# Splitting two operand sums before they go through memory, and adding the residual by DMA

## The chip, the cores and the metric

The kernel runs on one core of a Trainium2 chip. The metric is the device time of one execution in microseconds (us). TensorE (PE) multiplies, VectorE (DVE) and ScalarE (ACT) work on tiles, GpSimd (POOL) and SyncE (SP) here mostly issue DMA transfers between the core's memory and the chip's.

## The reference, cut to what matters

The block is a mixer (a state-space branch and a short convolution, merged by gates) with a residual, a norm, and then an MLP with a squared ReLU, a residual and a final norm. The change is in the MLP and its residual.

```
h = h + mixer_block(rmsnorm(h, g1), ...)
xn = rmsnorm(h, g2)                         # 1024 x 1024
f = relu(xn @ w_ff1); f = f * f             # 1024 x 4096
h = h + f @ w_ff2                           # 1024 x 1024
out = rmsnorm(h, g_final)
```

## The kernel before

All tensors are float32. TensorE works on the faster fp32r type, so each operand is cut into a high part (a rounded copy made by ScalarE) and a low part (the operand minus the high part, made by VectorE), and a product is three matmuls: high by high, high by low, low by high.

The MLP's two products are computed in **groups** by a scheme of the Strassen kind: a group multiplies a 2x2 block of weights by a 2x2 block of the operand with seven block products P1 to P7 instead of eight. One block product is a **chain** of 12 matmuls of 128x512 (4 blocks of the inner dimension, three matmuls each). Groups 0 to 13 belong to the first product, groups 14 to 25 to the second, and one slab of the inner dimension is multiplied in the plain way, in 16 chains (`pf`) between group 13 and group 14. The last stage (`pl`) adds another plain slab, the residual, and the final norm.

`seven(g, after)` issues one group in the order P1, P4 of the group before, P5, P2, P6, P3, P7. P1 is copied by ScalarE into the bank `seed` with its sign turned, and P6, P7 and P4 add to it there. Results leave the banks as quadrants in `done`: c11 after P2, c12 after P3, c22 after P7, c21 after P4. P4 writes into the bank that c22 is read from, so it waits for VectorE's c22. Behind each chain `after(i)` is called (i from 0 to 6), which issues the cutting and loading that other groups need. Each engine runs its own instructions in the order in which the program issues them; nothing else sets the order.

The weights of a group come as two raw tiles (`group_load`, SP). `w_parts` forms two sums of them (steps s1, s2), their high parts (h0 to h3) and low parts (l0 to l3); the tables `FIRST` and `SECOND` say behind which chain of the group before (first list) and of the group itself (second list) each step is issued. In the first product, sum 1 serves P5 and P6, sum 2 serves P3 and P7, part 0 serves P1 and P2, part 3 serves P4. In the second product part 0 serves P2 and P4.

The squared quadrants of the first product are the operands of the second: B11, B12, B21, B22 and the sums t1, n2, t3, t4 formed from them in `done`. POOL stores each to memory (`out_of`, 256 KB each) and SP loads it back per chunk of four groups (`x_load`, two loads of 512 KB each per name); `x_cut` cuts it (two ScalarE copies, two VectorE subtractions of 128x1024). The second product has three chunks; a boundary between chunks lies at groups 17 to 18 and 21 to 22. The residual h lies in memory as `hd`, written long before; eight tiles `ha` are loaded from it ahead of the plain slab, and every quadrant of the second product is added into them by VectorE.

In the rows, gs, gh and gl are a group's sum, high and low part, ha the accumulated output, xl1B and the like low parts of the second product's operands (the digit is the chunk), fh and fl those of a plain slab, hw and lw those of a plain slab's weights, holda, holdb, holdc the tiles for quadrants and sums of the first product.

Of the kernel before, what the change touches and what calls it, by code (L numbers as in the profile page):

```python
# [39 lines left out]


X_OF = {"P1": "B11", "P5": "t1", "P2": "B21", "P6": "n2", "P3": "B22", "P7": "t3", "P4": "t4"}


@with_exitstack
def block_kernel(ctx, tc, x_t, par, ssm, w_u, win, wco, wglu, wo, w1, w2, out):
# [632 lines left out]
    def ssm_z():  # L679
# [31 lines left out]
    hd = [dram.tile([P, S], F32, tag=f"hd{i}", name=f"hd{i}") for i in range(8)]  # L711
    h2d = {i: dram.tile([P, S], F32, tag=f"h2d{i}", name=f"h2d{i}") for i in range(8 * N_CHUNK, DFF // P)}
    xd = {
        (q, nm): dram.tile([P, 4, HALF], F32, tag=f"xd{q}{nm}", name=f"xd{q}{nm}")
        for q in range(N_CHUNK) for nm in X_OF.values()
    }

    def load_x(i):
# [276 lines left out]
    def four(t):  # L995
        return t.rearrange("p (a k m) -> p a k m", a=2, k=4)
# [29 lines left out]
    def w_parts(g):  # L1026

        (r0, r1), w = gw[g]["raw"], gw[g]
        second = g >= N_GROUP
        a11, a22 = r0[:, 0], r1[:, 1]  # L1030
        a12, a21 = (r1[:, 0], r0[:, 1]) if second else (r0[:, 1], r1[:, 0])
        full, single = (r1, a11) if second else (r0, a22)
        src = {"0": full, "3": single}
        of = {"1": ("P5", "P6"), "2": ("P3", "P7"), "0": ("P2", "P4") if second else ("P1", "P2"),
              "3": ("P1",) if second else ("P4",)}
        hi, lo = {}, {}

        def tile_for(kind, nm):
            if nm == "3":
                return half(f"g{kind}3_{g}", F32R).rearrange("p (k m) -> p k m", k=4)  # L1040
            return (u4 if second and nm != "1" else l4)(f"g{kind}{nm}_{g}")

        def sums(nm):
            t = four(unit(f"gs{nm}_{g}")) if g == 0 else wpool.tile(
                [P, 8, P], F32, tag="w", name=f"gs{nm}_{g}").rearrange("p (a k) m -> p a k m", a=2)
            src[nm] = t
            if nm == "1":
                V.tensor_add(t[:, 0], a21, a22)
                V.tensor_add(t[:, 1], t[:, 0], a11)
            else:  # L1050
                V.tensor_add(t[:, 0], src["1"][:, 1], a12)
                V.tensor_add(t[:, 1], a11, a21)  # L1052

        def high(nm):
            hi[nm] = tile_for("h", nm)
            A.activation(hi[nm], src[nm], AF.Copy)  # L1056

        def lower(nm):
            lo[nm] = tile_for("l", nm)
            V.tensor_sub(lo[nm], src[nm], hi[nm].bitcast(F32))  # L1060
            for i, name in enumerate(of[nm]):
# [8 lines left out]
                gw[g]["do"]["shl".index(what[0])](what[1])  # L1070
            yield

    FIRST = ["s1 h0", "s2 h1 l0", "h2 l1", "l2"], ["", "", "h3", "l3"]
    SECOND = ["", "", "", "s1 h3", "h1 l3", "l1"], ["s2 h0", "l0 h2", "l2"]

    def group_steps(g, own):
# [51 lines left out]
        next(rms[1])  # L1128

    def group_first():  # L1130
        next(prep0)
        next(prep0)

    group_load(0)
    prep0 = group_steps(0, 0)
# [39 lines left out]
    xq = {}  # L1175

    def x_load(q, name):
        ts = []
        for u in range(2):
            t = unit(f"xl{q}{name}{u}", F32R)  # L1180
            nc.sync.dma_start(t.bitcast(F32), xd[q, name][:, 2 * u:2 * u + 2, :].rearrange("p k t -> p (k t)"))
            ts.append(t)
        xq[q, name] = ts

    def x_cut(q, name):
        ops = []
        for u, t in enumerate(xq[q, name]):
            hi = unit(f"xh{q}{name}{u}", F32R)
            A.activation(hi, t.bitcast(F32), AF.Copy)
            low.append((t, t.bitcast(F32), hi))  # L1190
            lows(1)
            ops.append((hi, t))
        lows()
        xq[q, name] = ops
# [4 lines left out]
    def seven(g, after):  # L1199

        seed = seeds[g % 2]
        pa, pe = bank(f"pa{g}"), bank(f"pe{g}")
        chain(pa, g, "P1", True)
        A.activation(seed, pa, AF.Copy, scale=-1.0)  # L1204
        after(0)
        if g not in (0, N_GROUP):
            last_product(g - 1)
        after(1)
        chain(pe, g, "P5", True)
        s5, v2 = half(f"s5_{g}"), half(f"v2_{g}")  # L1210
# [12 lines left out]
        done(g, "c22", seed, s5)
        after(6)
# [7 lines left out]
    def done(g, quad, ps, less):  # L1232
# [8 lines left out]
        paired = g >= 2  # L1241
        q, c = divmod(g - 2, 4)

        def out_of(name, t):
            nc.gpsimd.dma_start(xd[q, name][:, c, :], t)

        hold = held.setdefault(g, {})
        if paired and quad == "c11":
# [21 lines left out]
        if quad == "c12":  # L1270
            t1 = hold["b"][:, HS[0]]
            V.tensor_sub(t1, hold["a"][:, HS[0]], t)
            out_of("t1", t1)
        elif quad == "c22":
            t3, n2 = hold["b"][:, HS[1]], hold["c"][:, HS[1]]
            V.tensor_sub(t3, hold["a"][:, HS[1]], t)
            out_of("t3", t3)
            V.tensor_sub(n2, hold["a"][:, HS[0]], t3)
            out_of("n2", n2)
        elif quad == "c21":  # L1280
            t4 = half(f"t4_{g}")
            V.tensor_sub(t4, t, hold["c"][:, HS[1]])
            out_of("t4", t4)

    plain_slab = 2 * N_CHUNK

    for g in range(N_GROUP):
        last_g = g == N_GROUP - 1
        if g == 0:
            for _ in prep0:  # L1290
                pass
        preps = [group_steps(g, 1), group_steps(g + 1, 0) if not last_g else iter(())]

        def after(i):
            for prep in preps:
                next(prep, None)
            if i == 4 and g + 2 < N_GROUP:
                group_load(g + 2)
            if last_g:
                if i == 2:  # L1300
                    slab_load(plain_slab)
                elif 3 <= i:
                    slab_cut(plain_slab, i - 3)
                if i == 4:
                    w2_cut(4 * plain_slab)

        seven(g, after)
    last_product(N_GROUP - 1)


    h = []
    for e in range(8):
        t = late.tile([P, S], F32, tag="l", name=f"ha{e}")
        nc.sync.dma_start(t, hd[e])
        h.append(t)

    names_x = list(X_OF.values())
    g0 = N_GROUP
# [1 line left out]
    for j in range(16):  # L1320
        n, ii, hh = 4 * plain_slab + j // 4, (j // 2) % 2, j % 2
        if j % 4 == 0 and j < 12:
            w2_cut(n + 1)
        if j == 9:
            group_load(g0)
            prep = group_steps(g0, 0)
        e = 2 * (j // 4) + ii
        p = bank(f"pf{n}_{ii}_{hh}")
        products(p, w2p[n], range(4 * ii, 4 * ii + 4), slab[plain_slab], HS[hh])
        V.tensor_add(h[e][:, HS[hh]], p, h[e][:, HS[hh]])  # L1330
        if j % 2 and j < 12:
            x_load(0, names_x[j // 2])
            if j > 1:
                x_cut(0, names_x[j // 2 - 1])
        if j >= 10:
            next(prep, None)
    group_load(g0 + 1)

    for g in range(g0, g0 + 4 * N_CHUNK):
        q, e = divmod(g - g0, 4)  # L1340
# [3 lines left out]
        def after(i):  # L1344
            if e == 0:
                if q == 0:
                    if i == 0:
                        x_cut(0, "t3")
                        x_load(0, "t4")
                    elif i == 2:  # L1350
                        x_cut(0, "t4")
                elif i == 0:
                    x_cut(q, "B22")
                elif i == 1:
                    x_load(q, "t4")
                elif i == 2:
                    x_cut(q, "t3")
                elif i == 4:
                    x_cut(q, "t4")
            if e == 3 and not final:  # L1360
                if i != 1:
                    x_load(q + 1, names_x[max(i - 1, 0)])
                if i >= 3:
                    x_cut(q + 1, names_x[i - 3])
            if final:
                if i == 0:
                    slab_load(n_slab - 1)
                if i in (2, 4):
                    for k in range(3) if i == 2 else (3,):
                        n = 4 * (n_slab - 1) + k  # L1370
                        w2p[n] = raw_load(w2[n], f"w2_{n}")
                if i >= 2:
                    if i < 6:
                        slab_cut(n_slab - 1, i - 2)
                    if i > 2:
                        n = 4 * (n_slab - 1) + i - 3
                        w2p[n] = cut(w2p[n], f"w2_{n}", blocks8)
            for prep in preps:
                next(prep, None)
            if i == 6:  # L1380
# [106 lines left out]
```

## Time and profile before

| what | value |
|---|---|
| median of 3 runs | 1485.74 us (1485.54 to 1486.83) |
| profiled execution | 1487.28 us, of which the span from the first to the last instruction is 1485.5 us |
| busy in the span | PE 1450.2 us (98%), DVE 1008.4 (68%), ACT 545.1 (37%), POOL 131.3 (9%) |
| mean granted TensorE clock | 0.991 |
| traffic | 144.31 MB, mean 97 GB/s |

Busy time is the sum over an engine's instructions. A PE that is busy can still be slow, since the granted clock stretches a matmul; the clock is given as a share of full speed.

### The profile page before, as it was taken

How to read it: one execution, taken by the hardware profiler on the slowest of the kernel's cores; microseconds unless marked ns; L12 is line 12 of the kernel's file. 1: busy time of each engine (PE TensorE's matmuls, PEld its weight loads, DVE VectorE, ACT ScalarE, POOL GpSimd, SP SyncE). 2: the span in 40 equal slices, each digit the busy share in tenths (PEclk: the TensorE clock that was granted, in tenths of full speed). 3: DMA queues.
4: the chain of work that ended last, by engine and by line, in shares of the span. 5: the costliest groups of instructions: out<-in, count | busy, mean ns of one | idle time of the engine just before them, and what ended most of it. 6: DMA issues, size and time to landing. Idle time of an engine off the chain costs nothing.

```text
span 1485.5 us, 16929 instructions
## 1 busy us (share of the span) xinstructions
PE 1450.2 (98%) x6563; PEld 1200.9 (81%) x6563; DVE 1008.4 (68%) x1573; ACT 545.1 (37%) x776; POOL 131.3 (9%) x306
## 2 busy tenths in 40 slices
PE   9989999999999999999999999999999999998997
PEld 7868888888888888888888878888887787887887
DVE  6678487776877776347536866766666657767565
ACT  6541432223232238324213443333324224344354
POOL 5840000000000000000010001222111000000000
PEclk9999999999999999999999999999999999999999
DMA  5111111101111111114312233444458516162302
GB/s 215 29 43 43 43 43 50 48 32 56 43 43 43 43 43 35 65 57 156 135 43 94 78 105 123 153 156 148 151 169 347 169 53 232 57 217 94 114 28 87
DMA packets 44096, 144.31 MB, mean 97 GB/s; under 512 B 5488, under 2 KB 9968, under 8 KB 44016
## 3 DMA queue, kind: packets, MB, share of 16 engines
q1 hardware_dynamic: 34736, 112.82, 22.6%
q0 software_dynamic: 9280, 30.42, 5.3%
q8 instruction: 51, 0.84, 0.2%
q14 instruction: 29, 0.24, 0.1%
HBM read 108.61 MB, written 34.60 MB: 96 GB/s over the span
## 4 chain that ended last, share of the span: by engine, by line
PE 83%; DVE 9%; ACT 4%; DMA 2%; issue 2%; SPq 0%; DVEq 0%; ACTq 0%
PE ps L134 8%; PE ps L136 8%; PE ps L135 8%; PE seed L1088 4%; PE seed L1090 4%; PE seed L1089 4%; PE pa L1090 3%; PE pa L1089 3%; PE pa L1088 3%; PE pe L1090 3%; PE pe L1089 3%; PE pe L1088 3%; PE pc L134 2%; PE pg L136 2%; PE pg L135 2%; PE pc L136 2%
## 5 line engine op out<-in xcount | busy, mean ns | idle before, releaser
L134 PE MATMUL ps<-xh,wh 128*128 128x512 f32 x656 | 259.8, 396 | 1.2 <-ACT wh L94 1.2
L136 PE MATMUL ps<-xh,wl 128*128 128x512 f32 x656 | 256.1, 390 | 2.2 <-DVE wl L95 2.2
L135 PE MATMUL ps<-xl,wh 128*128 128x512 f32 x656 | 255.3, 389 | 0.0
L136 PEld LDWEIGHTS ps<-xh,wl 128*128 128x128 f32 x656 | 123.1, 188 | 29.8 <-DVE wl L95 3.9
L134 PEld LDWEIGHTS ps<-xh,wh 128*128 128x128 f32 x656 | 123.3, 188 | 28.6 <-ACT wh L94 2.3
L135 PEld LDWEIGHTS ps<-xl,wh 128*128 128x128 f32 x656 | 123.2, 188 | 25.3
L95 DVE TENSOR_TENSOR wl<-wr,wh 128x1024 fp32r<-128x1024 f32 x57 | 70.1, 1230 | 59.0 <-ACT wh L94 59.0
L94 ACT ACTIVATE wh<-wr 128x1024 fp32r<-128x1024 f32 x57 | 59.6, 1047 | 52.3 <-PE pc L135 21.0
L1204 ACT ACTIVATE seed<-pa 128x512 f32<-128x512 f32 x26 | 15.1, 582 | 160.2 <-PE pa L1090 160.2
L893 POOL DMA_DIRECT2D hd<-h x16 | 8.9, 559 | 711.5 <-ACT ssum L895 636.4
L1060 DVE TENSOR_TENSOR gl<-gs,gh 128x1024 fp32r<-128x1024 f32 x52 | 63.3, 1219 | 0.0
L1056 ACT ACTIVATE gh<-gs 128x1024 fp32r<-128x1024 f32 x52 | 54.7, 1052 | 22.5 <-DVE gs L1052 11.7
L134 PE MATMUL pc<-vh,wh 128*128 128x512 f32 x128 | 49.9, 390 | 0.0
L134 PE MATMUL pw<-mh,hwo 128*128 128x512 f32 x128 | 49.9, 390 | 0.0
L136 PE MATMUL pc<-vh,wl 128*128 128x512 f32 x128 | 49.8, 389 | 0.0
L136 PE MATMUL pw<-mh,lwo 128*128 128x512 f32 x128 | 49.8, 389 | 0.0
L135 PE MATMUL pw<-ml,hwo 128*128 128x512 f32 x128 | 49.8, 389 | 0.0
L134 PE MATMUL pg<-zh,wh 128*128 128x512 f32 x128 | 49.8, 389 | 0.0
L135 PE MATMUL pg<-zl,wh 128*128 128x512 f32 x128 | 49.8, 389 | 0.0
L136 PE MATMUL pg<-zh,wl 128*128 128x512 f32 x128 | 49.8, 389 | 0.0
L135 PE MATMUL pc<-vl,wh 128*128 128x512 f32 x128 | 49.8, 389 | 0.0
L1060 DVE TENSOR_TENSOR gl<-rg,gh 128x1024 fp32r<-128x1024 f32 (+1 forms) x52 | 49.5, 952 | 0.0
(518 smaller groups left out, 3565.6 us busy)
## 6 DMA issues: line engine op xcount, KB each, us to landing
rg<-in_w SPq DMA_DIRECT2D x52, 512.0 KB, 3.6
wr<-in_win SPq DMA_DIRECT2D x41, 512.0 KB, 3.5
wr<-in_wco SPq DMA_DIRECT2D x8, 512.0 KB, 3.5
wr<-in_wglu SPq DMA_DIRECT2D x8, 512.0 KB, 3.5
rwo<-in_wo SPq DMA_DIRECT2D x8, 512.0 KB, 6.8
h<-in_x_t SPq DMA_DIRECT2D x8, 512.0 KB, 7.5
hd<-h POOLq DMA_DIRECT2D x16, 256.0 KB, 2.3
fl<-h2d SPq DMA_DIRECT2D x8, 512.0 KB, 4.3
```

Source lines behind the costliest of these rows:

```text
L94: A.activation(hi, r, AF.Copy)
L95: V.tensor_sub(lo, r, hi.bitcast(F32))
L134: T.matmul(ps, wh[:, j, :], xh[:, cols], start=start and i == 0, stop=False)
L135: T.matmul(ps, wh[:, j, :], xl[:, cols], start=False, stop=False)
L136: T.matmul(ps, wl[:, j, :], xh[:, cols], start=False, stop=stop and i == n - 1)
L893: nc.gpsimd.dma_start(hd[i][:, c], h[i][:, c])
L1056: A.activation(hi[nm], src[nm], AF.Copy)
L1060: V.tensor_sub(lo[nm], src[nm], hi[nm].bitcast(F32))
L1088: T.matmul(p, wh[:, kb, :], xh, start=first and kb == 0, stop=False, skip_group_check=True)
L1089: T.matmul(p, wh[:, kb, :], xl, start=False, stop=False, skip_group_check=True)
L1090: T.matmul(p, wl[:, kb, :], xh, start=False, stop=kb == 3, skip_group_check=True)
L1204: A.activation(seed, pa, AF.Copy, scale=-1.0)
```

## The change

Five things are changed. Of the seven operands of the second product, t1 and n2 are cut into high and low parts already in the first product, by `split_out`, and go through memory as two parts; `x_cut` then does nothing for them. The low part is issued at the next `after`. The table `FIRST` moves the weight steps: sum 2 and its parts are issued within the group itself, and for group 0 everything in the group-before list is issued in `plain(0, 0)`. The eight residual loads are gone from SP; ScalarE copies the plain slab's sums into `ha`, and POOL adds `hd` to them by eight accumulating DMAs of 512 KB in groups 15 and 16. The loads and cuts of chunk 0's operands and of the last plain slab's weights stand at other places (`last_cut`). The last slab's weights are cut behind P7 and P4 of group 25 (lw_28 behind P7, the other three behind P4) instead of between that group's chains. Two pre-loads are issued at other points of a group, and the copies s5 and v2 of the first product share a tile of another pool.

```diff
+SPLIT = ("t1", "n2")
...
         (q, nm, part): dram.tile([P, 4, HALF], F32, ...)
         for q in range(N_CHUNK) for nm in X_OF.values() for part in ("hl" if nm in SPLIT else "r")
...
-    FIRST = ["s1 h0", "s2 h1 l0", "h2 l1", "l2"], ["", "", "h3", "l3"]
+    FIRST = ["", "", "s1 h0", "l0 h1", "l1"], ["s2 h2", "l2", "h3", "l3"]
...
     def group_first():
-        next(prep0)
-        next(prep0)
+        for _ in prep0:
+            pass
...
     def x_load(q, name):
...
+        got = []
+        for part in "hl" if name in SPLIT else "r":
+            for u in range(2):
...
     def x_cut(q, name):
+        if name in SPLIT:
+            return
...
-        s5, v2 = half(f"s5_{g}"), half(f"v2_{g}")
+        if g < N_GROUP:
+            sv = late.tile([P, S], F32, tag="l", name=f"sv{g}")
+            s5, v2 = (sv[:, c] for c in HS)
+        else:
+            s5, v2 = half(f"s5_{g}"), half(f"v2_{g}")
...
+        def split_out(name, t, lo=None):
+            hi = half(f"h{name}_{g}", F32R)
+            A.activation(hi, t, AF.Copy)
+            out_of(name, hi.bitcast(F32), "h")
+            def rest():
+                V.tensor_sub((t if lo is None else lo).bitcast(F32R), t, hi.bitcast(F32))
+                out_of(name, t if lo is None else lo, "l")
+            waiting.append(rest)
...
-            out_of("t1", t1)
+            split_out("t1", t1)
...
+            V.tensor_sub(n2, hold["a"][:, HS[0]], t3)
             out_of("t3", t3)
-            V.tensor_sub(n2, hold["a"][:, HS[0]], t3)
-            out_of("n2", n2)
+            split_out("n2", n2, half(f"ln2_{g}"))
...
             for prep in preps:
                 next(prep, None)
-            if i == 4 and g + 2 < N_GROUP:
+            while waiting:
+                waiting.pop(0)()
+            if i == 6 and g + 2 < N_GROUP:
                 group_load(g + 2)
             if last_g:
-                if i == 2:
+                if i == 0:
                     slab_load(plain_slab)
...
     for e in range(8):
-        t = late.tile([P, S], F32, tag="l", name=f"ha{e}")
-        nc.sync.dma_start(t, hd[e])
-        h.append(t)
+        h.append(late.tile([P, S], F32, tag="l", name=f"ha{e}"))
...
-        V.tensor_add(h[e][:, HS[hh]], p, h[e][:, HS[hh]])
-        if j % 2 and j < 12:
-            x_load(0, names_x[j // 2])
-            if j > 1:
-                x_cut(0, names_x[j // 2 - 1])
+        A.activation(h[e][:, HS[hh]], p, AF.Copy)
+        if j % 3 == 1:
+            x_load(0, names_x[j // 3])
+        if j % 3 == 0 and 0 < j < 15:
+            x_cut(0, names_x[j // 3 - 1])
...
+    def last_cut(k):
+        n = 4 * (n_slab - 1) + k
+        w2p[n] = cut(w2p[n], f"w2_{n}", blocks8)
...
                 if q == 0:
                     if i == 0:
-                        x_cut(0, "t3")
+                        x_load(0, "t3")
+                        x_cut(0, "B22")
+                    elif i == 1:
                         x_load(0, "t4")
-                    elif i == 2:
-                        x_cut(0, "t4")
...
+            if q == 0 and e in (1, 2) and 1 <= i <= 4:
+                k = 4 * (e - 1) + i - 1
+                nc.gpsimd.dma_start(h[k], hd[k], accum_op=ALU.add)
...
-                if i >= 3:
+                if i in (3, 5):
                     x_cut(q + 1, names_x[i - 3])
...
-                if i >= 2:
-                    if i < 6:
-                        slab_cut(n_slab - 1, i - 2)
-                    if i > 2:
-                        n = 4 * (n_slab - 1) + i - 3
-                        w2p[n] = cut(w2p[n], f"w2_{n}", blocks8)
+                if 2 <= i < 6:
+                    slab_cut(n_slab - 1, i - 2)
+                if i == 6:
+                    last_cut(0)
...
     last_product(g0 + 4 * N_CHUNK - 1)
+    for k in range(1, 4):
+        last_cut(k)
```

VectorE in the stage ahead of group 0, where the first sums of group 0's weights are formed (gs_0, gl_0), before:

```order
L1048 TENSOR_TENSOR gs_0_6145<-rg_1_6100 128x512
L1049 TENSOR_TENSOR gs_0_6145<-gs_0_6145,rg_0_6098 128x512
L1051 TENSOR_TENSOR gs_0_6150<-gs_0_6145,rg_0_6098 128x512
L1052 TENSOR_TENSOR gs_0_6150<-rg_0_6098,rg_1_6100 128x512
L1060 TENSOR_TENSOR gl_0_6155<-rg_0_6098,gh_0_6148 128x1024
L968 TENSOR_TENSOR f_0_6159<-r_0_6157 128x512
```

and after:

```order
L1049 TENSOR_TENSOR gs_0_6151<-rg_1_6106 128x512
L1050 TENSOR_TENSOR gs_0_6151<-gs_0_6151,rg_0_6104 128x512
L1061 TENSOR_TENSOR gl_0_6156<-rg_0_6104,gh_0_6154 128x1024
L1061 TENSOR_TENSOR gl_0_6160<-gs_0_6151,gh_0_6158 128x1024
L969 TENSOR_TENSOR f_0_6164<-r_0_6162 128x512
```

The second sum has moved behind, into group 0, and the low part of the first sum (the second gl_0) has come ahead of f_0; before, it stood some 60 instructions further on.

VectorE at the boundary of groups 17 and 18, from the cut of chunk 1's B21 to the second weight sum of group 18, before:

```order
L930 TENSOR_TENSOR xl1B_9253<-xl1B_9253,xh1B_9313 128x1024
L930 TENSOR_TENSOR xl1B_9255<-xl1B_9255,xh1B_9315 128x1024
L1060 TENSOR_TENSOR gl_18_9319<-gs_18_9263,gh_18_9291 128x1024
L1237 TENSOR_TENSOR ha_8489<-seed_6434,ha_8489 128x512
L1239 TENSOR_TENSOR ha_8489<-ha_8489,s_17_9231 128x512
L930 TENSOR_TENSOR xl1n_9281<-xl1n_9281,xh1n_9339 128x1024
L930 TENSOR_TENSOR xl1n_9283<-xl1n_9283,xh1n_9341 128x1024
L930 TENSOR_TENSOR xl1B_9309<-xl1B_9309,xh1B_9364 128x1024
L930 TENSOR_TENSOR xl1B_9311<-xl1B_9311,xh1B_9366 128x1024
L1051 TENSOR_TENSOR gs_18_9370<-gs_18_9263,rg_1_9176 128x512
```

and after (the operands' tiles are now called xr where they are cut, and line numbers are 9 or 1 higher):

```order
L931 TENSOR_TENSOR xr1B_9353<-xr1B_9353,xh1B_9411 128x1024
L931 TENSOR_TENSOR xr1B_9355<-xr1B_9355,xh1B_9413 128x1024
L1061 TENSOR_TENSOR gl_18_9417<-gs_18_9363,gh_18_9389 128x1024
L1246 TENSOR_TENSOR ha_8582<-seed_6439,ha_8582 128x512
L1248 TENSOR_TENSOR ha_8582<-ha_8582,s_17_9327 128x512
L931 TENSOR_TENSOR xr1B_9407<-xr1B_9407,xh1B_9456 128x1024
L931 TENSOR_TENSOR xr1B_9409<-xr1B_9409,xh1B_9458 128x1024
L1052 TENSOR_TENSOR gs_18_9462<-gs_18_9363,rg_1_9272 128x512
```

The first xl1B pair is B21 and the second B22; the pair xl1n between c22's two instructions on ha and B22 is gone. Further ahead the pair xl1t of t1 is gone too.

VectorE at the end of group 13, the first product's last, from the plain slab's low part fl_1 to c22 (holdc<-seed), before:

```order
L1168 TENSOR_TENSOR fl_1_8362<-fl_1_8362,fh_1_8403 128x1024
L736 TENSOR_TENSOR lw_24_8409<-rw_24_8406,hw_24_8408 128x1024
L1263 TENSOR_TENSOR holda_8380<-pe_8309,v_13_8356 128x512
L1152 SCALAR_TENSOR_TENSOR holda_8380<-holda_8380 128x512
L1272 TENSOR_TENSOR holdb_8424<-holda_8380 128x512
L1168 TENSOR_TENSOR fl_2_8364<-fl_2_8364,fh_2_8429 128x1024
L1263 TENSOR_TENSOR holdc_8444<-seed_6434,s_13_8355 128x512
```

and after:

```order
L1169 TENSOR_TENSOR fl_1_8415<-fl_1_8415,fh_1_8494 128x1024
L737 TENSOR_TENSOR lw_24_8500<-rw_24_8497,hw_24_8499 128x1024
L1283 TENSOR_TENSOR holda_8471<-pe_8394,sv_8455 128x512
L1153 SCALAR_TENSOR_TENSOR holda_8471<-holda_8471 128x512
L1292 TENSOR_TENSOR holdb_8515<-holda_8471 128x512
L1263 TENSOR_TENSOR holdb_8515<-holdb_8515,ht_13_8519 128x512
L1169 TENSOR_TENSOR fl_2_8417<-fl_2_8417,fh_2_8524 128x1024
L1283 TENSOR_TENSOR holdc_8539<-seed_6439,sv_8455 128x512
```

A subtraction on holdb has come in ahead of fl_2: the low part of t1, which reads ScalarE's ht_13. On ScalarE ht_13 stands ahead of fh_2, the high part that fl_2 reads.

## Rows read from the trace of the kernel before

**Rows 1.** Waits of TensorE: engine, line, waited for, us in total, times, longest.

```profile
PE seed L1088 <- DVE ha L1237: 6.8, 3, 2.8
PE pa L1090 <- DVE gl L1060: 4.5, 3, 2.1
PE pe L1090 <- DVE gl L1060: 3.4, 1, 3.4
PE seed L1088 <- DVE holdc L1263: 2.6, 1, 2.6
```

**Rows 2.** Windows, first matmul of a chain to another's first; the last two are wider.

```profile
core 0: us, PE busy (x) PEld busy (x) DVE busy (x) ACT busy (x) POOL busy (x), PEclk, DMA share, GB/s
859.61:867.58 7.97, 4.60 (x13) 3.32 (x12) 7.83 (x12) 4.09 (x5) 0.54 (x1) 0.79 0.18 68
1123.27:1131.62 8.35, 5.72 (x25) 4.43 (x24) 8.18 (x11) 2.12 (x3) 1.94 (x4) 1.00 1.02 406
1177.87:1188.38 10.51, 7.59 (x25) 5.47 (x24) 7.31 (x8) 7.39 (x9) 0.00 (x0) 0.84 0.62 204
1253.69:1269.33 15.64, 13.11 (x50) 9.99 (x48) 14.73 (x17) 9.74 (x12) 0.00 (x0) 0.89 0.52 183
1334.66:1354.37 19.71, 15.84 (x61) 12.24 (x60) 18.26 (x20) 9.45 (x12) 0.00 (x0) 0.91 0.47 173
1414.21:1424.33 10.12, 7.33 (x25) 5.58 (x24) 7.42 (x9) 2.81 (x3) 0.00 (x0) 0.83 0.00 0
...
1249.00:1258.00 9.00, 7.57 (x34) 5.94 (x32) 8.58 (x11) 8.41 (x10) 0.00 (x0) 1.00 1.02 409
...
880.00:1100.00 220.00, 220.00 (x972) 182.21 (x972) 150.88 (x203) 75.68 (x107) 41.29 (x76) 1.00 0.43 147
```

**Rows 3.** Timeline of TensorE: start, us, instruction, in brackets the wait before it.

```profile
1258.72 0.50 PE L1088 MATMUL seed<-xh0t,gh 128*128 128x512 f32 x1 [2.15 <-DVE ha L1237]
```

**Rows 4.** Timeline of VectorE ahead of group 0 and in it.

```profile
821.78 1.22 DVE L1060 TENSOR_TENSOR gl<-rg,gh 128x1024 fp32r<-128x1024 f32 x1
...
862.32 2.36 DVE L1060 TENSOR_TENSOR gl<-gs,gh 128x1024 fp32r<-128x1024 f32 x2
```

**Rows 5.** Timeline of VectorE at the boundary of groups 17 and 18.

```profile
1250.37 2.36 DVE L930 TENSOR_TENSOR xl1t<-xl1t,xh1t 128x1024 fp32r<-128x1024 f32 x2 [0.35 <-ACT xh1t L1189]
...
1257.98 0.69 DVE L1237 TENSOR_TENSOR ha<-seed,ha 128x512 f32<-128x512 f32 x1
1258.70 0.69 DVE L1239 TENSOR_TENSOR ha<-ha,s 128x512 f32<-128x512 f32 x1
1259.31 2.35 DVE L930 TENSOR_TENSOR xl1n<-xl1n,xh1n 128x1024 fp32r<-128x1024 f32 x2
...
1265.66 1.22 DVE L1060 TENSOR_TENSOR gl<-rg,gh 128x1024 fp32r<-128x1024 f32 x1
```

**Rows 6.** Timeline of VectorE and ScalarE at the end of group 13.

```profile
1126.30 0.69 DVE L1272 TENSOR_TENSOR holdb<-holda 128x512 f32<-128x512 f32 x1
1126.91 1.22 DVE L1168 TENSOR_TENSOR fl<-fl,fh 128x1024 fp32r<-128x1024 f32 x1
1128.04 0.69 DVE L1263 TENSOR_TENSOR holdc<-seed,s 128x512 f32<-128x512 f32 x1
...
1121.00 0.60 ACT L1217 ACTIVATE v<-seed 128x512 f32<-128x512 f32 x1 [1.42 <-DMA xd2B<-c]
...
1123.39 2.00 ACT L1167 ACTIVATE fh<-fl 128x1024 fp32r<-128x1024 f32 x2
```

**Rows 7.** Timeline of VectorE in group 25.

```profile
1413.27 1.23 DVE L1168 TENSOR_TENSOR fl<-fl,fh 128x1024 fp32r<-128x1024 f32 x1 [0.21 <-ACT fh L1167]
...
1418.01 1.22 DVE L736 TENSOR_TENSOR lw<-rw,hw 128x1024 fp32r<-128x1024 f32 x1
1419.15 0.68 DVE L1237 TENSOR_TENSOR ha<-seed,ha 128x512 f32<-128x512 f32 x1
```

**Rows 8.** DMA issues: count, size, median us to landing.

```profile
rg<-in_w SPq DMA_DIRECT2D x52, 512.0 KB, 3.6
...
ha<-hd SPq DMA_DIRECT2D x8, 512.0 KB, 11.0
...
xd1t<-holdb POOLq DMA_DIRECT2D x8, 256.0 KB, 2.7
```

More of the change, by code (lines that the diff above doesn't have):

```diff
@@ L713, in block_kernel @@
     xd = {
-        (q, nm): dram.tile([P, 4, HALF], F32, tag=f"xd{q}{nm}", name=f"xd{q}{nm}")
-        for q in range(N_CHUNK) for nm in X_OF.values()
+        (q, nm, part): dram.tile([P, 4, HALF], F32, tag=f"xd{q}{nm}{part}", name=f"xd{q}{nm}{part}")
+        for q in range(N_CHUNK) for nm in X_OF.values() for part in ("hl" if nm in SPLIT else "r")
     }
@@ L1043, in sums @@
         def sums(nm):
-            t = four(unit(f"gs{nm}_{g}")) if g == 0 else wpool.tile(
+            t = four(unit(f"gs{nm}_{g}")) if g == 0 and nm == "1" else wpool.tile(
                 [P, 8, P], F32, tag="w", name=f"gs{nm}_{g}").rearrange("p (a k) m -> p a k m", a=2)
@@ L1177, in x_load @@
     def x_load(q, name):
[L1178 to L1183, printed above, removed]
+        got = []
+        for part in "hl" if name in SPLIT else "r":
+            for u in range(2):
+                t = unit(f"x{part}{q}{name}{u}", F32R)
+                src = xd[q, name, part][:, 2 * u:2 * u + 2, :]
+                nc.sync.dma_start(t.bitcast(F32), src.rearrange("p k t -> p (k t)"))
+                got.append(t)
+        xq[q, name] = got if len(got) == 2 else list(zip(got[:2], got[2:]))
     def x_cut(q, name):
+        if name in SPLIT:
+            return
         ops = []
@@ L1242, in done, with out_of @@
         q, c = divmod(g - 2, 4)
-        def out_of(name, t):
-            nc.gpsimd.dma_start(xd[q, name][:, c, :], t)
+        def out_of(name, t, part="r"):
+            nc.gpsimd.dma_start(xd[q, name, part][:, c, :], t)
+        def split_out(name, t, lo=None):
[6 more added lines that the diff above has]
+            waiting.append(rest)
         hold = held.setdefault(g, {})
@@ L1283, in done @@
             out_of("t4", t4)
+    waiting = []
     plain_slab = 2 * N_CHUNK
@@ L1288, in block_kernel @@
         last_g = g == N_GROUP - 1
-        if g == 0:
-            for _ in prep0:
-                pass
         preps = [group_steps(g, 1), group_steps(g + 1, 0) if not last_g else iter(())]
@@ L1308, in block_kernel @@
     last_product(N_GROUP - 1)
+    while waiting:
+        waiting.pop(0)()
     h = []
     for e in range(8):
-        t = late.tile([P, S], F32, tag="l", name=f"ha{e}")
-        nc.sync.dma_start(t, hd[e])
-        h.append(t)
+        h.append(late.tile([P, S], F32, tag="l", name=f"ha{e}"))
     names_x = list(X_OF.values())
@@ L1355, in after @@
                     x_load(q, "t4")
-                elif i == 2:
+                if i == 2:
                     x_cut(q, "t3")
```

## The prediction

> **What bounds the kernel now.** I began with the busy shares: TensorE is busy for 1450.2 of 1485.5 us, so only what stops or slows it can be won. The waits of TensorE come next [rows 1]: in the MLP, four lines carry nearly all of them, 6.8 us on VectorE's additions into ha, 4.5 and 3.4 on low parts of weights (gl), 2.6 on holdc. A wait is not the whole loss, because the granted clock can fall behind it. So I took, from the timeline, the stretch from the last chain that ran on time to the first that did so again, and read its length against the number of chains in it [rows 2]. In a long undisturbed stretch 972 matmuls take 220.00 us at clock 1.00 [rows 2], 0.2263 us each, so a chain of 12 takes 2.72 us. That gives six places:
>
> a, group 0, P5 (859.61): 7.97 us for 1 chain, loss 5.25.
> e, end of group 13, P7 and P4 (1123.27): 8.35 for 2 chains, loss 2.91.
> b, group 14, P5 and P2 (1177.87): 10.51 for 2, loss 5.07.
> c, groups 17 to 18 (1253.69): 15.64 for 4, loss 4.76.
> d, groups 21 to 22 (1334.66): 19.71 for 5, loss 6.11.
> f, end of group 25 (1414.21): 10.12 for 2, loss 4.68.
>
> The sum is 28.8 us, all that the change can win. The granted clock is 0.79 to 0.91 over five of these stretches, but 1.00 over e [rows 2], so waits of 2 us and more were followed by the half clock (1.2 instead of 2.4 GHz) in most places, not in all.
>
> **Term a: +5.25.** P5 of group 0 waits for the low part of sum 1. It is made at 862.32 us [rows 4], behind the operand sums of the first product, although its inputs were there 40 us earlier. In the new order it follows the first low part in the stage ahead. There the second sum's two additions are gone and one low part has come in, so it ends near 823 us: the row at 821.78 [rows 4] is the first low part now, which moves ahead by those two additions, and its own 1.22 us takes their place. Sum 2 moves into group 0, where P3 wants it, three chains behind P5 (8.2 us). The whole loss goes; I see no cover for it that would vanish.
>
> **Term c and d: +3.65 and +5.0.** P4 waits for c22's addition into ha, which VectorE starts at 1257.98 [rows 5], and TensorE starts at 1258.72 after a wait of 2.15 [rows 3]. P4's place is one chain behind 1253.69, at 1256.41. Ahead of the addition VectorE loses the pair of low parts of t1 at 1250.37, which occupies 2.27 us start to start in a full queue (2.36 by the row) [rows 5]. So the addition ends at 1258.67 − 2.27 = 1256.40, and P4 is late by 0 to 0.3. The pair of n2 at 1259.31 [rows 5] goes as well. The low part gl at 1265.66, for which P2 waits, then comes 2 x 2.27 earlier and ends near 1262.3 at best; P2's third matmul wants it at 1253.69 + 3 x 2.72 + 0.45 = 1262.3. B22's pair still stands ahead of it, and c21's addition, which follows P4, too, so I allow 0.8 there. With 0.3 + 0.8 = 1.1 left, c gains 4.76 − 1.1 = 3.65 and d, with the same order, 6.11 − 1.1 = 5.0. Bounds: 0 to 2.2 left at each. Waits this short I price at full clock.
>
> Behind it stands a cost: the operands now come in 18 loads per chunk instead of 14. In 1249 to 1258 us transfers already run at share 1.02 and 409 GB/s [rows 2]. Four more loads of 0.524 MB take 4 x 0.524/409 = 5.1 us in such a stretch. The loads start in the last group of the chunk as tiles come free, in the order of use, so the 5.1 us falls on t3 and t4, wanted several chains after B11; I take nothing and keep it as a rival.
>
> **Term f: +3.7.** Three cuts of plain weights stand ahead of c22's addition in group 25, one of them at 1418.01, and the addition starts at 1419.15 [rows 7]. They move behind it. Then VectorE has fl_1, fl_2 at 1413.27 [rows 7], c12's two instructions and fl_3, and the addition follows P7's end (1414.21 + 2.72 = 1416.93) by about 0.2, ends near 1417.85, and P4 is 0.9 late instead of its loss of 4.68. The moved cuts are wanted by the last stage 3.6 us later, and by steps of 2.8 us for 1.22 us of work, so they are hidden. Bounds 2.0 (half clock stays) to 4.4.
>
> **Term e: −3.2.** Here the change adds. VectorE's low part of t1 comes between holdb at 1126.30 and fl at 1126.91 [rows 6]. It reads ScalarE's high part of t1, which can only start when t1 is done, 1126.95, and takes 0.60, by the row at 1121.00 [rows 6] of the same shape. Then the low part runs to 1128.2. On ScalarE fh_2 now stands behind that high part; a 128x1024 copy takes 1.0 (2.00 for 2 at 1123.39) [rows 6], so it ends at 1128.5, and fl_2 runs from there for 1.14. Then c22's subtraction starts near 1129.65 instead of 1128.04 [rows 6]: P4 is 1.6 later. A wait of 2.6 + 1.6 = 4.2 us is longer than any behind which the clock stayed up [rows 1, 2], so the half clock should follow: at f the loss of 4.68 is a wait of 2.8 [rows 1] and 1.9 behind it; I take 1.6 for it. Together 3.2; bounds 0, if VectorE has other slack, and 3.2.
>
> **Term b: 0.** The order there is ScalarE's copy of P1, two high parts of an operand, then the weights' high part; VectorE two low parts, then sum 2 and gl. Another operand (B22 for t3) takes the same place, with the same shapes.
>
> **Residual: 0.** Eight loads leave SP at the start of the plain slab, and VectorE's 16 additions of about 0.65 us become ScalarE copies; neither engine bounds that stretch. Eight accumulating DMAs of 512 KB are new on POOL, which issues nothing else there. With T the start of P1 of group 15, the third (h[2]) is issued behind c11's addition at T + 11.8, since P2 is the fourth chain (4 x 2.72 and the addition), and the other five directly behind it. c12's addition of group 15 must wait for the third, c22's (h[3]) for the fourth. VectorE is in order: behind them queue the next group's sums and lows, and P4 waits for c22. It must end by T + 21.76 (8 chains), so start by T + 20.4. With r us each, one after another, the fourth lands at T + 12.3 + 2r: no loss up to r = 4.05. The trace has no accumulating DMA. From below: a POOL store of 256 KB lands in 2.7, and another 256 KB at 409 GB/s add 0.64: 3.3; an SP load of 512 KB takes 3.6. From above: 11.0, the eight loads of hd side by side [rows 8]. I take 3.3 to 3.6, the same kind of issue and size, and no loss.
>
> The Trainium skill (DMA: Bandwidth & Descriptors, Rules for kernel authors) says that an accumulating DMA reads its destination and writes it later, and that any other access of those bytes has to wait for its semaphore. By that rule the waits of c12 and c22 are real and can't overlap the transfer; no run so far shows one. The same page (Anatomy of one DMA) puts a POOL-issued transfer at 2.0 us plus its bytes over 436 thousand per us; my estimate by it for 512 KB is 3.2 us, so by that too the term would be 0.
>
> **Steady state of the first product: 0.** In 880 to 1100 us VectorE is busy 150.88 of 220 [rows 2], 13.1 us per group of 7 chains (19.04). Two more subtractions of about 0.6 per group make 14.3, ScalarE gains two copies, POOL two stores; all fit.
>
> **Sum.** 5.25 + 3.65 + 5.0 + 3.7 − 3.2 = +14.4. The profiled execution took 1487.28 (span 1485.5); it becomes 1472.9. Its time is 1.54 above the median of 1485.74, so the median becomes **1471.3**. Own range by the bounds: gains of 10.2 (5.0 + 2.5 + 3.9 + 2.0 − 3.2) to 20.5 (5.25 + 4.76 + 6.1 + 4.4), 1465.2 to 1475.5.
>
> **Rivals.** (1) *The boundaries give nothing.* The 5.1 us of extra loads delays B21 or B22, so c22 and gl stay late. For it: share 1.02; against it: the late instructions are behind VectorE's queue, not DMA, at c. Loses 8.65: 1480.0. (2) *The accumulating DMAs hold VectorE up, other side.* For it: nothing prices them; at r the loss is the largest of 2r − 8.1 (group 15), 4r − 27.1 (group 16, another 19.04 later) and 6r − 46.2 (group 17). It outweighs 14.4 from r = 10.1 on; at 11.0 [rows 8] it is 19.9: 1491.2. Against it: those 11.0 us are eight transfers sharing one stretch. (3) *e costs nothing and the boundaries are wholly won*: 20.5, 1465.2. (4) *The change doesn't act*: the waits come from somewhere that the order leaves as it is, 1485.7; a speaks against it.
>
> **Numbers.** Chances: forecast 0.54, rival 1 0.2, rival 2 0.08, rival 3 0.13, rival 4 0.05. Range 1465 to 1482, from rival 3 to a little over rival 1; left out are rivals 2 and 4 and edges. A difference of 0.2% (3 us) is about what a measurement can tell from no change: faster 0.86, same 0.05, slower 0.09.
>
> **What would show it.** Right: no wait for gl in group 0; TensorE's waits for ha near 1 us or less at the boundaries and in group 25; P4 of group 13 waiting longer, over 3.5 us; b as before; accumulating DMAs landing under 4 us. Wrong: c22 of groups 15 to 17 waiting on a POOL DMA; loads of B21 or B22 as the releaser of ScalarE at 17 and 21; new waits in groups 1 to 12.

## The result, and the profile after

The changed kernel takes 1471.62 us (median of 4 runs, 1470.70 to 1472.24), the kernel before beside it 1485.64: a ratio of 0.9909, 95% interval 0.9892 to 0.9926. Forecast were 1471.3 and the range 1465 to 1482. Its profiled execution took 1471.11 us, with a span of 1469.3 at clock 0.995.

The waits of TensorE after, against [rows 1] (engine, line, waited for, us in total, times, longest):

```profile
PE seed L1089 <- DVE holdc L1283: 4.2, 1, 4.2
PE pa L1091 <- DVE gl L1061: 3.4, 3, 2.1
...
PE pa L1089 <- ACT gh L1057: 0.8, 1, 0.8
PE seed L1089 <- DVE ha L1246: 0.8, 1, 0.8
```

The wait of P5 for gl is gone, the 6.8 us for ha are 0.8 in that line, and the wait for holdc at the end of group 13 has grown from 2.6 to 4.2. The second of these rows is two waits of 0.6 us at c and d and one of 2.1 at b. The same six places as windows, from the start of a chain to the start of another, against [rows 2]:

```profile
858.18:860.90 2.72, 2.72 (x13) 2.25 (x12) 2.72 (x6) 1.12 (x2) 0.54 (x1) 1.00 0.25 96
1116.58:1128.92 12.34, 8.17 (x26) 6.20 (x24) 9.91 (x13) 3.15 (x4) 3.25 (x6) 0.74 0.84 271
1175.43:1184.38 8.95, 6.03 (x25) 4.35 (x24) 5.75 (x6) 7.01 (x9) 0.00 (x0) 1.00 0.91 326
1249.66:1261.94 12.28, 11.51 (x49) 8.85 (x48) 10.63 (x13) 7.40 (x9) 0.00 (x0) 1.00 0.99 361
1327.23:1339.51 12.28, 11.51 (x50) 8.86 (x48) 10.63 (x13) 7.40 (x9) 0.00 (x0) 1.00 1.00 382
1402.13:1408.67 6.54, 5.76 (x26) 4.42 (x24) 5.23 (x7) 3.75 (x4) 0.00 (x0) 1.00 0.00 0
```

With a chain at 2.716 us (d holds 4 chains now, since the fifth runs on time) the losses are these:

| place | before | after | gain | forecast |
|---|---|---|---|---|
| a, group 0 | 5.25 | 0.0 | +5.25 | +5.25 |
| e, end of group 13 | 2.9 | 6.9 | −4.0 | −3.2 |
| b, group 14 | 5.1 | 3.5 | +1.6 | 0 |
| c, groups 17 to 18 | 4.8 | 1.4 | +3.4 | +3.65 |
| d, groups 21 to 22 | 6.1 | 1.4 | +4.7 | +5.0 |
| f, end of group 25 | 4.7 | 1.1 | +3.6 | +3.7 |
| sum | 28.8 | 14.3 | +14.5 | +14.4 |

The table compares one execution of each kernel, and a place can cost more or less from one execution to the next (last section). The medians differ by 14.0. The two profiled executions differ by 16.2; of the rest, 1.4 us lie ahead of group 0, where P5 began at 859.61 and now at 858.18 (the windows' bounds).

### The profile page after: what moved, and what is told of

It reads as the page before. It is cut to its first block, busy times and chain, and to the rows that moved or that the text cites. A ratio compares the mean times of both kernels' runs of the same rounds, so it can differ in the third digit from the quotient of the medians.

```text
span 1469.3 us, 17037 instructions
## 1 busy us (share of the span) xinstructions
PE 1442.7 (98%) x6563; PEld 1195.8 (81%) x6563; DVE 998.4 (68%) x1569; ACT 557.0 (38%) x804; POOL 150.4 (10%) x338
## 4 chain that ended last, share of the span: by engine, by line
PE 88%; DVE 6%; ACT 4%; issue 1%; DMA 1%; SPq 0%; DVEq 0%; ACTq 0%
PE ps L135 8%; PE ps L137 8%; PE ps L136 8%; PE seed L1089 5%; PE seed L1091 5%; PE seed L1090 5%; PE pa L1091 3%; PE pa L1089 3%; PE pa L1090 3%; PE pe L1091 3%; PE pe L1089 3%; PE pe L1090 3%; PE pc L135 2%; PE pg L137 2%; PE pc L136 2%; PE pg L135 2%
## 5 line engine op out<-in xcount | busy, mean ns | idle before, releaser
L1089 PE MATMUL seed<-xht,gh 128*128 128x512 f32 x112 | 44.7, 399 | 4.2 <-DVE holdc L1283 4.2
```

The costliest lines, as they stand in the source:

```text
L1089: T.matmul(p, wh[:, kb, :], xh, start=first and kb == 0, stop=False, skip_group_check=True)
```

## The experiments

All times are medians beside runs of the kernel before on the same chip (1484.5 to 1485.2). Losses by place are worked out as above, in the profiled execution of each kernel.

**FIRST alone.** The kernel before with the new table, sum 2's tile, `group_first` and the load's point.

```diff
...
-    FIRST = ["s1 h0", "s2 h1 l0", "h2 l1", "l2"], ["", "", "h3", "l3"]
+    FIRST = ["", "", "s1 h0", "l0 h1", "l1"], ["s2 h2", "l2", "h3", "l3"]
...
```

> The kernel before with the new table FIRST alone (with the tile of sum 2, the whole group-before list of group 0 in the stage ahead, and the load of two groups ahead behind P7). Theory: P5 of group 0 no longer waits for the low part of sum 1, the 5.25 us of that place go and nothing else moves: 1480.4 us. Rival 1: the wait only moves to P3, which wants sum 2: 1483 to 1486. Rival 2: the freed VectorE time also shortens other places of the first product's end: under 1478.

1482.06 us, ratio 0.9968 (0.9954 to 0.9983). That is 2.5 to 6.8 us, in which 5.25 lies. In its windows a has lost its loss, and e, where the order is that of before, now shows clock 0.83 instead of 1.00:

```profile
857.68:860.40 2.72, 2.72 (x13) 2.25 (x12) 2.72 (x6) 1.12 (x2) 0.54 (x1) 1.00 0.25 96
1116.09:1126.22 10.13, 7.31 (x25) 5.60 (x24) 8.79 (x11) 2.30 (x3) 2.17 (x4) 0.83 1.03 406
```

The theory's place is confirmed, and no other chain of group 0 waits, so rival 1 is out. The median is 1.7 us over the theory's 1480.4. In the profiled execution (1483.36 us, the slowest of ten) e lost 4.7 instead of 2.9 (10.13 us for 2 chains) behind nearly the same wait (2.8 us against 2.6), and c lost 6.1 instead of 4.8; that would account for the shortfall, but what the other nine executions lost there isn't shown.

**No split.** The changed kernel with t1 and n2 stored whole.

```diff
-SPLIT = ("t1", "n2")
+SPLIT = ()
...
-            split_out("t1", t1)
+            out_of("t1", t1)
...
-                if i in (3, 5):
+                if i >= 3:
```

> The changed kernel with t1 and n2 again stored whole and cut after the load. Theory: the cuts queued on VectorE ahead of c22 and of the low part of the weights are the whole of the losses at groups 17 to 18 and 21 to 22, so these go from 1.4 back to 4.8 and 6.1, and the end of group 13 from 7.1 back to about 2.9: 1471.6 + 3.4 + 4.7 - 4.2 = 1475.5. Rival: the boundaries are eased by the new places of loads and cuts, not by the split, and stay at 1.4: 1467.4.

1479.86 us (1474.97 to 1482.28), ratio 0.9962 (0.9949 to 0.9976). Windows at e, b, c and d:

```profile
1115.75:1125.45 9.70, 7.32 (x26) 5.57 (x25) 8.35 (x11) 1.87 (x2) 2.17 (x4) 0.82 0.73 227
1171.68:1181.61 9.93, 7.01 (x26) 5.05 (x24) 6.72 (x7) 7.38 (x9) 0.00 (x0) 0.89 0.91 319
1247.53:1264.21 16.68, 12.83 (x49) 9.79 (x48) 15.82 (x17) 9.45 (x12) 0.00 (x0) 0.92 0.50 189
1329.83:1349.57 19.74, 15.89 (x62) 12.25 (x61) 18.28 (x20) 9.44 (x12) 0.00 (x0) 0.91 0.44 164
```

The losses at c and d are back, 16.68 − 4 x 2.716 = 5.8 and 19.74 − 5 x 2.716 = 6.2, so the rival (1467.4) is out: the split is what eased the boundaries. The total was missed by 4.4 us, and the places account for it when b and c are read one chain further, to where the half clock ends: e loses 4.3 where 2.9 was expected, b 5.1 where 3.5, c 6.1 where 4.8. At c the half clock came behind P2's wait for gl (2.0 us) and not, as in the profile before, behind P4's wait for c22. So the 4.8 of c was that execution's; d, where the clock fell behind P2 in both, lost 6.1 before and 6.2 here.

**Cuts back.** The changed kernel with the last weights cut between the chains of group 25.

```diff
-                if i == 6:
-                    last_cut(0)
+                if i > 2:
+                    last_cut(i - 3)
...
-    for k in range(1, 4):
-        last_cut(k)
```

> The changed kernel with the cuts of the last four plain weights back between the chains of group 25. Theory: c22's addition comes behind three of them again, P4 of group 25 waits near 2.8 us and the half clock follows, loss 4.7 instead of 1.1: 1475.2. Rival: what eased that place is something else (the group loads' new point, the accumulated output ready earlier): 1471.6.

1473.98 us (1472.01 to 1475.55). TensorE's wait at f is back (2.8 us for ha in this line), and its window:

```profile
PE seed L1089 <- DVE ha L1246: 2.8, 1, 2.8
```

```profile
1403.00:1412.74 9.74, 6.95 (x26) 5.29 (x24) 7.42 (x9) 2.81 (x3) 0.00 (x0) 0.87 0.00 0
```

It loses 4.3 against 1.1. In the total that is +2.4, with a ratio (0.9919, 0.9900 to 0.9939) whose interval overlaps that of the changed kernel; the place is clearer, and the rival would have left the wait away.

**Residual loaded.** The changed kernel with SP's eight loads and VectorE's additions.

```diff
...
+        nc.sync.dma_start(t, hd[e])
...
-        A.activation(h[e][:, HS[hh]], p, AF.Copy)
+        V.tensor_add(h[e][:, HS[hh]], p, h[e][:, HS[hh]])
...
-                nc.gpsimd.dma_start(h[k], hd[k], accum_op=ALU.add)
```

> The changed kernel with the residual loaded by SP ahead of the plain slab and the plain sums added to it by VectorE; no accumulating DMA. Theory: the residual's way is worth nothing, VectorE's and SP's work there lies beside TensorE's: 1471.6, within 1 us; VectorE's wait of 4.1 us for a DMA in group 15 goes without effect. Rival 1: the eight loads on SP and 16 additions delay chunk 0's operands, and the plain slab or group 14 waits: over 1473.5. Rival 2: the accumulating DMAs cost something through VectorE's wait: under 1470.

1470.63 us (1469.54 to 1472.82), ratio 0.9899 (0.9880 to 0.9919) against 0.9909: no difference. In the total the residual's new way is worth nothing that these runs can tell, as forecast. One place does differ:

```profile
PE seed L1089 <- DVE holdc L1283: 5.2, 1, 5.2
```

SP runs ahead and issues the eight loads from 1101.91 us on, inside group 13, and P4 of that group waits 5.2 us here, against 4.2 in all six profiles that have the changed kernel's order at that place. Ahead of it ScalarE's copy of P2's result waits 3.6 us for the store of n2's high part, 2.2 in the changed kernel. Neither rival named this cost. Read one chain further, the place loses 7.4 against 7.2, since the half clock behind the wait was shorter, and b loses 5.1 here, by the clock.

**Weights first.** The changed kernel, s2 h0 and l0 h2 ahead of B22's cut.

```diff
         def after(i):
+            if e == 0 and i == 0:
+                next(preps[0], None)
+                next(preps[0], None)
             if e == 0:
```

> The changed kernel with the first two weight steps of a chunk's first group (s2 h0, l0 h2) issued ahead of the cut of B22 instead of behind it. Theory: at group 14 the operand's two high parts on ScalarE and two low parts on VectorE are what P2 waits for, 3.5 us there and 0.8 at each of groups 18 and 22; all go: 1471.6 - 5.1 = 1466.5. Rival 1: the cut of B22, now later, holds up P3: 1470 or more. Rival 2: the weights' parts wait for the raw weights' loads, not for the order: 1471.6.

1467.38 us (1465.49 to 1468.14). Group 14's stretch is whole, 5.47 us for 2 chains; the second window is group 15, 20.25 us for 7 chains (19.01), where c22 of group 14 comes late now:

```profile
1175.07:1180.54 5.47, 5.47 (x26) 4.44 (x25) 3.03 (x3) 5.27 (x7) 0.00 (x0) 1.00 0.95 347
1188.69:1208.94 20.25, 19.61 (x85) 15.61 (x84) 12.14 (x18) 5.27 (x7) 5.33 (x6) 1.00 0.72 149
```

So b was an order on ScalarE and VectorE; of 5.1 us expected 4.2 came, since 1.2 is lost at the new wait; P2's waits at c and d are gone, 0.95 us each with what followed them.

**Residual twice.** Each accumulating DMA is issued twice; the output holds the residual twice.

```diff
                 nc.gpsimd.dma_start(h[k], hd[k], accum_op=ALU.add)
+                nc.gpsimd.dma_start(h[k], hd[k], accum_op=ALU.add)
```

> The changed kernel with each of the eight accumulating DMAs issued twice, so that the output holds the residual twice. Theory: each takes 2.8 us more behind another, VectorE's c22 of group 15 had 0.5 us to spare, so it now comes some 5 us late, P4 of group 15 waits as long, the half clock may follow, and one wait of this kind is all: 1476 to 1480. Rival 1: transfers overlap and the residual stays hidden: 1471.6. Rival 2: the queue on POOL piles up so that groups 16 and 17 wait as well: over 1482.

1500.73 us (1496.91 to 1503.00), ratio 1.0107 (1.0079 to 1.0136): my expectation missed, and the time is that of rival 2, though the waits are not where it put them. On POOL the second of a pair waits for the first (brackets), and the next pair stands behind it:

```profile
1198.27 1.18 POOL L1387 DMA_DIRECT2D ha<-hd  x1
1207.73 0.87 POOL L1388 DMA_DIRECT2D ha<-hd  x1 [8.28 <-DMA ha<-hd]
1208.34 1.16 POOL L1387 DMA_DIRECT2D ha<-hd  x1
1216.06 0.86 POOL L1388 DMA_DIRECT2D ha<-hd  x1 [6.56 <-DMA ha<-hd]
```

VectorE's c12 of group 15, and what TensorE waited for it in all:

```profile
1221.55 0.69 DVE L1246 TENSOR_TENSOR ha<-pe,ha 128x512 f32<-128x512 f32 x1 [17.39 <-DMA ha<-hd]
```

```profile
PE seed L1089 <- DVE ha L1246: 25.0, 3, 18.2
```

The 18.2 us are P4 of group 15, 6.0 are P4 of group 17; P4 of group 16 doesn't wait, and the third wait is the 0.8 of group 25.

A pair takes some 8.3 us (1207.73 to 1216.06), so 4.2 per transfer. I had priced only the transfers of h[2] and h[3]; those of h[0] and h[1] now hold POOL until 1208.34, 6 us behind the end of c11's addition (1202.23), at which h[2] was free. It is the prediction's rival 2, with its mechanism: c12 and c22 queued behind a DMA.

**End of group 13.** The changed kernel with the plain slab's cuts and t1's low part moved in group 13.

```diff
-            while waiting:
+            while waiting and not (last_g and i == 5):
...
-                elif 3 <= i:
-                    slab_cut(plain_slab, i - 3)
+                elif i in (2, 3):
+                    slab_cut(plain_slab, i - 2)
...
+                elif i == 6:
+                    slab_cut(plain_slab, 2)
+                    slab_cut(plain_slab, 3)
```

> The changed kernel with the plain slab's cuts in group 13 moved: two of them one chain earlier, two behind P7, and the low part of t1 of that group behind P7 too. Theory: c22's subtraction then follows P7's end at once, P4 of group 13 is late by about 1 instead of 7.1 us with the clock: 1471.6 - 6.0 = 1465.6, and the clock stays up there. Rival 1: the first plain chain waits instead for the two cuts that moved back: 1469 to 1471. Rival 2: with the clock up at this place it falls at group 14, as it did before the change, and takes back 1.6: 1467.2.

1467.61 us (1465.33 to 1469.13). Windows at e and b:

```profile
1114.35:1120.91 6.56, 5.78 (x25) 4.43 (x24) 5.72 (x10) 1.36 (x3) 1.62 (x3) 1.00 0.85 267
1168.31:1178.61 10.30, 7.38 (x26) 5.39 (x25) 7.10 (x8) 7.39 (x9) 0.00 (x0) 0.83 0.91 310
```

P4's place loses 1.1 instead of 6.9; the first plain chain then loses 1.1, waiting for fl. The clock fell at b (10.30 for 2 chains, 4.9): rivals 1 and 2 both took a part, and the total is near rival 2's.

**Both.** The two edits together.

```diff
+            if e == 0 and i == 0:
...
+                elif i in (2, 3):
```

> Both of the two preceding edits. Theory: they are at different places and add up, 5.1 + 6.0: 1460.5. Rival: one stall hides part of the other (a late group 14 gave the loads time): 1462 or more.

1463.11 us (1462.19 to 1464.13), ratio 0.9849 (0.9827 to 0.9872): 8.5 us under the changed kernel, where 11.1 were expected. The parts that were short above (1.2 in group 15, 1.1 behind P4 of group 13) are short here too; no other stall came in.

**The changed kernel twice more.** No edit.

> The changed kernel once more, for one question: is the loss of 3.5 us at group 14, against 5.1 before, the change's or the clock's chance? Theory: the waits there (0.8 for gh, 2.1 for gl) are the same each time, and the clock behind them either falls or not, in any kernel: in this run the place costs 3.5 or 5.1. Rival: the change itself keeps the clock up there: 3.5 in each run of it.

> As the run before it: the changed kernel once more. Theory: the waits of group 14 are again 0.8 and 2.1, and the place costs 3.5 or 5.1 by the clock; at the end of group 13 a wait of 4.2 is followed by the half clock each time. Rival: 3.5 again.

1471.44 and 1472.68 us. The waits at b are the same, and the windows:

```profile
1175.11:1184.05 8.94, 6.02 (x26) 4.35 (x24) 5.74 (x6) 7.00 (x9) 0.00 (x0) 1.00 0.93 312
```

```profile
1177.06:1185.96 8.90, 5.98 (x25) 4.35 (x24) 5.70 (x6) 6.96 (x9) 0.00 (x0) 1.00 0.88 316
```

3.5 both times, as the rival had it; at the end of group 13 both waited 4.2 us again, with the half clock behind it. The kernel with the cuts back, which has the changed kernel's instructions up to group 25, lost 3.5 at b as well. But the kernel with the residual twice runs the changed kernel's instructions up to group 14, and its window there is

```profile
1171.75:1182.11 10.36, 7.44 (x26) 5.35 (x25) 7.16 (x8) 7.39 (x9) 0.00 (x0) 0.85 0.87 304
```

10.36 for 2 chains, 4.9, at clock 0.85. So the change's order alone doesn't keep the clock up there; what did, in four of these five executions, stays open.

**Early additions.** Both edits, and the accumulating DMAs issued earlier.

```diff
-            if q == 0 and e in (1, 2) and 1 <= i <= 4:
-                k = 4 * (e - 1) + i - 1
-                nc.gpsimd.dma_start(h[k], hd[k], accum_op=ALU.add)
+            if q == 0 and e in (1, 2) and i == 1:
+                for k in ((2, 3, 0, 1), (4, 5, 6, 7))[e - 1]:
+                    nc.gpsimd.dma_start(h[k], hd[k], accum_op=ALU.add)
```

> The kernel with both edits (weights first, end of group 13), and the accumulating DMAs of h[2] and h[3] issued ahead of those of h[0] and h[1], all four behind P4 of group 14, and the next four together one group later. Theory: they no longer wait for c11 of group 15, VectorE's wait of 4 us for them goes, but since it lay just within the time to spare the total stays that of the kernel with both edits, 1463.1 within 1.5. Rival: they now start in group 14, beside the loads of t3 and t4, and P7 or P4 of group 14 waits: 1465 or more.

1461.95 us (1460.12 to 1463.92), ratio 0.9845 (0.9820 to 0.9869): the same as both edits, within 1.5. POOL issues h[2] and h[3] in the plain slab now, and VectorE waits for no accumulating DMA. This is the fastest kernel of the study.

## Why the prediction was right, by its own steps

**Term a** was right to the hundredth, and FIRST alone shows that it belongs to the table.

**Terms c and d** were right in mechanism and close in size. VectorE at c after the change:

```profile
1251.95 0.68 DVE L1246 TENSOR_TENSOR ha<-seed,ha 128x512 f32<-128x512 f32 x1
1252.67 0.69 DVE L1248 TENSOR_TENSOR ha<-ha,s 128x512 f32<-128x512 f32 x1
1254.15 2.36 DVE L931 TENSOR_TENSOR xr1B<-xr1B,xh1B 128x1024 fp32r<-128x1024 f32 x2 [0.79 <-ACT xh1B L1194]
...
1258.24 1.21 DVE L1061 TENSOR_TENSOR gl<-rg,gh 128x1024 fp32r<-128x1024 f32 x1
```

c22's addition ends 2.97 us behind P1 of group 18 (1249.66), where [rows 5] had 4.98, and P4 began 0.3 late (1252.69), as assumed. B22's pair still stands ahead of gl; the 0.8 set aside for it was 0.8. The four loads more cost nothing: c and d run at DMA share 0.99 and 1.00 and have no wait for a load on their path, so rival 1 is out. Of the 1.4 us that are left at each, 0.3 are P4's lateness and 0.8 P2's; the other 0.3, for which the prediction had nothing, is the longer time of the matmuls just behind these two waits. And c's loss before, 4.8, was low by where the clock fell in that execution, as No split and FIRST alone show (6.1).

**Term f** came as worked out: loss 1.1 instead of 4.7.

**Term e** was right in mechanism and too small in one part. VectorE there, against [rows 6]:

```profile
1119.36 0.69 DVE L1292 TENSOR_TENSOR holdb<-holda 128x512 f32<-128x512 f32 x1
1120.81 0.69 DVE L1263 TENSOR_TENSOR holdb<-holdb,ht 128x512 fp32r<-128x512 f32 x1 [0.76 <-ACT ht L1259]
1121.75 1.23 DVE L1169 TENSOR_TENSOR fl<-fl,fh 128x1024 fp32r<-128x1024 f32 x1 [0.25 <-ACT fh L1168]
1122.89 0.68 DVE L1283 TENSOR_TENSOR holdc<-seed,sv 128x512 f32<-128x512 f32 x1
```

and TensorE's P4:

```profile
1123.63 0.79 PE L1089 MATMUL seed<-xht,gh 128*128 128x512 f32 x1 [4.17 <-DVE holdc L1283]
```

Against the start of P7 the subtraction begins at 6.31 (1122.89 − 1116.58), before at 4.77: 1.5 later, forecast 1.6. The half clock behind it was the part mis-sized: it lasted through all 12 matmuls of P4 (12.34 − 5.43 − 4.3 = 2.6, where 4.3 is the lateness of P4's start, 1123.63 − 1116.58 − 2.72), where I took 1.6 from f. Part of the 4.0 is the clock of the execution before, which stayed up at this place: against No split, where it fell there too, the split costs 2.6 (6.9 − 4.3).

**Term b** was forecast at 0, and 1.6 was gained. The waits are the same within a hundredth; the two of P2, before and after:

```profile
1181.56 0.50 PE L1088 MATMUL pa<-xh0B,gh 128*128 128x512 f32 x1 [0.81 <-ACT gh L1056]
1184.41 0.50 PE L1090 MATMUL pa<-xh0B,gl 128*128 128x512 f32 x1 [2.11 <-DVE gl L1060]
```

```profile
1179.12 0.50 PE L1089 MATMUL pa<-xh0B,gh 128*128 128x512 f32 x1 [0.80 <-ACT gh L1057]
1181.96 0.50 PE L1091 MATMUL pa<-xh0B,gl 128*128 128x512 f32 x1 [2.11 <-DVE gl L1061]
```

The difference is the clock, 1.00 against 0.84, and nothing in the prediction foresaw it. It was luck that the forecast's total came out so near: this 1.6 made up for e (0.8 too small) and c, d and f (0.25, 0.3 and 0.1 too large).

**Residual, 0**: right in the total, with the transfer's time mis-sized on the way. The accumulating DMAs and the additions that wait for them:

```profile
1204.95 2.66 POOL L1387 DMA_DIRECT2D ha<-hd  x3 [4.76 <-issue]
```

```profile
1210.31 0.69 DVE L1246 TENSOR_TENSOR ha<-pe,ha 128x512 f32<-128x512 f32 x1 [4.07 <-DMA ha<-hd]
...
1213.09 0.69 DVE L1246 TENSOR_TENSOR ha<-seed,ha 128x512 f32<-128x512 f32 x1 [0.17 <-DMA ha<-hd]
```

```profile
ha<-hd POOLq DMA_DIRECT2D x8, 512.0 KB, 7.4
```

The transfer of h[2] took 5.4 us from its issue, not 3.3 to 3.6, and the next landed 2.8 behind it. c22's addition ended at 1213.78, and P4 of group 15 was due at 1214.30 (1211.58 + 2.72): 0.5 us to spare. By the prediction's own rule (12.3 + 2r, to be there by 20.4) the two transfers, 8.1 us from the first one's issue to the second one's landing, took all of the 8.1 us allowed; the 0.5 is there because the rule left 1.36 us for c22, about both of its instructions, and P4 waits for the first alone. It is a narrow margin: in the first of the two repeats of the same kernel VectorE's c22 waited longer for the DMA, and P4 of group 15 came late:

```profile
1213.72 0.69 DVE L1246 TENSOR_TENSOR ha<-seed,ha 128x512 f32<-128x512 f32 x1 [1.03 <-DMA ha<-hd]
1214.46 0.50 PE L1089 MATMUL seed<-xh0t,gh 128*128 128x512 f32 x1 [0.34 <-DVE ha L1246]
```

That cost 0.6 us there. So rival 2's mechanism, priced at a chance of 0.08, did come, small, in one of the four executions with the same instructions there (Cuts back is the fourth); the kernel with the residual twice shows how large it can get. Of the signs that the prediction named, "landing under 4 us" failed (7.4 in the median), and c22 of group 15 did wait on a POOL DMA, which it had listed under wrong; neither cost more than this 0.6 us.

The term also took the old loads to lie where the program has them, at the start of the plain slab. SP ran ahead and issued them from 1109.20 us on, inside group 13; there they were not quite free, as the one profile of Residual loaded shows by 1.0 us more of P4's wait.

The rule of the Trainium skill (DMA: Bandwidth & Descriptors, Rules for kernel authors) that other accesses of the bytes have to wait for an accumulating DMA agrees with the trace, in VectorE's wait of 4.07 us. The estimate of 3.2 us by the formula of the same page of the Trainium skill (Anatomy of one DMA) doesn't: the fastest of the eight took 5.3 us, and the measurement decides.

**The first product's steady state, 0**, was right: no wait of TensorE lies between group 0 and the end of group 13.

## What to carry to other kernels

Where an engine is 98% busy, list the few places where it stops, count the work in each against its length, and follow one instruction there through its queue; here that gave six terms that came out within 1.6 us each. A queue that runs in order makes a piece of work dear or free by its place: the same cuts cost 3.2 us ahead of c22 (Cuts back, 4.3 against 1.1) and nothing that shows behind it, and t1's low part, an instruction of 0.7 us, with the high part that it waits for cost 2.6 to 4.0 us at the one place where P4 follows P7 at once. A transfer that adds into a tile should be issued as soon as the tile is free of earlier writers: with the early additions VectorE waits for none, while behind the later ones it stood 4.1 us, and 17.4 with each issued twice. In the total that was worth nothing here that these runs can tell.

## What the runs showed of the hardware that was not expected

The price of a wait varies with the clock behind it. The same instructions with the same wait were followed by the half clock in one execution and not in another: b in the changed kernel's order lost 3.5 us (clock 1.00) and 4.9 (0.85). With nearly the same instructions and wait, e in the order of before lost 2.9 (1.00) and 4.7 (0.83), and c lost 4.8 or 6.1 by which of its two waits the half clock followed. That is up to 1.8 us at a place, and so a sum of six such terms can't be known better than to a few microseconds.

The stage ahead of the MLP, which these edits leave nearly alone, ends at different times. P5 of group 0 began at 855.67 us in the kernel with the residual twice and at 859.81 in the one with both edits, although they run the same instructions until then; the first 10 us already differ, with 23 and 17 matmuls done:

```profile
0.00:10.00 10.00, 7.17 (x23) 5.23 (x24) 3.81 (x8) 5.25 (x7) 0.69 (x6) 1.00 0.77 268
```

```profile
0.00:10.00 10.00, 7.74 (x17) 5.30 (x18) 3.94 (x8) 5.39 (x7) 0.69 (x6) 1.00 0.77 256
```

So a difference between two single executions is worth little under 4 us, and the forecast's nearness to the median (0.3 us) owes something to chance.
